# Spreading the conditioning products and the combination of the dilated branch over twice as many token steps

## Chip, cores and metric

The kernel runs on one core of a Trainium2 chip. The metric is the device time of one execution in microseconds, and lower is better. All data are float32. Matrix products run as three passes over operands that are split into a high part (`whi`, `hT0`) and a low part (`wlo`, `hT1`).

## What is computed

The reference is one encoder layer with conditioning. A vector `c` gives, through one large product, six rows that scale, shift and gate the two halves of the layer. The first half normalises the input, projects it, runs two kinds of attention side by side, gates and merges them; the second half is a SwiGLU network. Cut to what matters here:

```python
c_act = jax.nn.silu(c)
mod = c_act @ w_ada[l] + b_ada[l]
sh1, sc1, gt1, sh2, sc2, gt2 = jnp.split(mod, 6, axis=-1)
h = rms_norm(x, g_norm1[l]) * (1.0 + sc1) + sh1
proj = h @ w_in[l]                       # q, k, v of both branches, and the gates
o_a = neighbourhood_attention(qa, ka, va, rpb[l])
# dilated branch: three groups (dilation 1, 4, 16), each with its log-denominator
wts = jax.nn.softmax(jnp.stack(lses, axis=0), axis=0)
o_b = jnp.einsum('gbsh,gbshd->bshd', wts, jnp.stack(outs, axis=0))
gate_a, gate_b = jnp.split(jax.nn.sigmoid(gates + b_gate[l]), 2, axis=-1)
merged = gate_a * (o_a @ w_proj_a[l]) + gate_b * (o_b @ w_proj_b[l])
x = x + gt1 * (merged @ w_o[l])
# second half: SwiGLU with sh2, sc2, gt2
```

## The kernel before

The projections of the attention branches are made in ten units of eight token tiles of 128 tokens each. The main loop runs over steps `n` from 6 to 91, with `u, t = divmod(n, 8)`: unit and token tile. Units 0 to 5 belong to the three groups of the dilated branch, units 6 to 9 (n = 48 to 79) are the fourth kind, the neighbourhood attention. From n = 58 (`PAIRED`) on, each step takes the scores of one attention item, the product with the values of the item before last, and the transposes of the item in between. Steps n = 80 to 91 have no projection any more; in its place stand twelve blocks of the gate product (`gate_pre`), two blocks (the two halves of the tokens) for each pair of weight tiles.

One step is issued in this order. Four chunks of the projection (line 305) or of the gates (line 704); the attention: scores (L468), products with the values (L509), transposes of queries and keys (L369), transposes of the probabilities (L494); four more chunks; then `ada_step`, `combine_step`, and the work behind the projection, `proj_post`, which stores the values to `v_d` (L345). At the last tile of a unit the values are loaded back with eight DMAs (L358).

- `ada_step` takes one of 64 products of the conditioning. It is made on DVE: a block of weights `wa` (512 KB for two products, L288) times a column is added to an accumulator (L292, L294). After every eighth product `ada_row` sums the accumulator over the partitions with a product with ones on PE (L271), DVE adds the bias (L275), and the row is stored to `mod_d` (L276).
- The combination of the dilated branch has twelve blocks. `combine_prep(i)` loads a block of attention results `ut` (L643, L646, L650) and lets DVE spread the weights into `fb` (L655, two instructions). `combine_step(i)` transposes `fb` on PE (L664, four transposes into a bank of the tag `t`), and DVE multiplies (L672, or L674 and L675 with a sum). After six blocks the result goes to `o_d` (L677).
- The weights of the gates are loaded with L111, 256 KB each, into `raw`; ACT makes the high part (L118) and POOL the low part (L119).

Two shared things decide what can overlap. The PSUM tag `t` has two banks: L494, L664 and L271 take turns in them, so a bank has to be emptied by DVE or ACT before the next of them can start. The SBUF tag `raw` has six buffers: the weights of the gates (L111), `ut`, `fb`, `row` and `brow` all take their turn in this one ring, in the order in which the program asks for them.

PE runs in the order in which the code is written. The other engines and the DMA queue of SP are put into an order by a planner with priorities; each then runs strictly in its order, and an instruction that waits holds up all that stand behind it.

Of the kernel before, what the change touches and what calls it, by code (L numbers as in the profile page):

```python
# [36 lines left out]
PAIRED, RBT, COMB = 58, 5, 64  # L37
# [6 lines left out]
def hybrid_layer(ctx: ExitStack, tc: tile.TileContext, x, colp, wada1, wada2, bada2, wqkv, wg, wpa, wpb,  # L44
# [30 lines left out]
    def bank(tag):  # L75
        return ps.tile([128, 512], F32, tag=tag, name="ps_" + tag)
# [37 lines left out]
    def wsplit(r, eng=None):  # L114
        n = r.shape[1]
        hi = wp.tile([128, 512], F32R, tag="hi", bufs=NHL, name="whi")
        lo = wp.tile([128, 512], F32R, tag="lo", bufs=NHL, name="wlo")
        nc.scalar.activation(hi[:, :n], r, AF.Copy)  # L118
        (eng or nc.gpsimd).tensor_sub(lo[:, :n], r, fview(hi[:, :n]))  # L119
        return hi, lo  # L120
# [59 lines left out]
    def unit_load(u, k):  # L180
        return wload(wqkv[u, :, k, :], 384)
# [84 lines left out]
    ada_state = {"i": 0}  # L266
# [33 lines left out]
    def proj_chunk(U, t, k):  # L300
        if k == 0:
            U.pd[t] = bank("d" if U.u else "t")
        pd = U.pd[t]
        for i, (a, b) in enumerate(PASS):
            nc.tensor.matmul(pd[:, :384], tok(a, k, t), U.w[k][b][:, :384],  # L305
                             start=(k == 0 and i == 0), stop=(k == KT - 1 and i == 2))
# [89 lines left out]
    def new_unit(u, w):  # L396
        U = Unit()
        U.kind, U.pair = UNITS[u]
        U.u = u
        U.w = w  # L400
        U.pd, U.qn = {}, {}
        qk = ap_.tile([128, 4, S], F32R, tag="qk", bufs=2, name="qk")
        U.qk = [qk[:, i, :] for i in range(4)]
        if U.kind == 0:
            U.v = big("v", [128, 8, 128])
        if U.kind < 3:
            U.tab = rtab[0] if rtab else None
            U.st = ap_.tile([128, 9, 4], F32, tag="st", bufs=2, name="st")
        else:
            U.bias = []  # L410
        return U
# [116 lines left out]
    def cl_scores(C):  # L528
        C.pS = [bank("s") for _ in range(2)]
        for I in C.items:  # L530
            U, nq, nk = I.U, I.nq, I.nkb * 128
            for i, (a, b) in enumerate(PASS):
                for h in range(2):
                    hs = slice(h * 64, h * 64 + 64)
                    nc.tensor.matmul(C.pS[h][:nq, I.c0:I.c0 + nk], U.qk[a][hs, I.q0:I.q0 + nq],
                                     U.qk[2 + b][hs, I.kb0 * 128:I.kb0 * 128 + nk], start=(i == 0), stop=(i == 2))
# [122 lines left out]
    def combine_step(i):  # L659
        pr, g, hf = i // 6, (i % 6) // 2, i % 2  # L660
        fb, ut, uv, acc = cb[i]
        pf = bank("t")
        for j in range(4):
            nc.tensor.transpose(pf[:, j * 128:(j + 1) * 128], fb[:, j].rearrange("p h d -> p (h d)"), ident)  # L664
        acc = acc[:, hf * 512:hf * 512 + 512]
        n = 1 if g == 0 else (4 if g == 1 else 8)

        def v(z):
            return z if g == 0 else z.rearrange("p (i r) -> p i r", r=n)

        if g == 0:
            nc.vector.tensor_mul(acc, ut, pf)  # L672
        else:
            nc.vector.tensor_mul(v(pf), uv, v(pf))  # L674
            nc.vector.tensor_add(acc, acc, pf)  # L675
        if g == 2 and hf == 1:
            nc.sync.dma_start(o_d[4 + pr], cb[i][3])  # L677
# [14 lines left out]
    def gate_pre(n):  # L692

        i, br, hf = n // 4, (n // 2) % 2, n % 2
        hs = slice(hf * 512, hf * 512 + 512)
        st = {}

        def chunk(k):
            if k == 0:
                gate_w(i, br)  # L700
                st["p"] = bank("d")
            j, kk = divmod(k, 4)
            for q, (a, b) in enumerate(PASS):
                nc.tensor.matmul(st["p"], gw[i, br][j][a][:, kk * 128:(kk + 1) * 128], hT[b][:, k, hs],  # L704
                                 start=(k == 0 and q == 0), stop=(k == 7 and q == 2))
            if k == 7:
                if hf == 0:
                    gsig[i, br] = big("gsig")
                dst = gsig[i, br][:, hs]
                nc.scalar.activation(dst, st["p"], AF.Identity, bias=bg_c[:, 8 * br + i:8 * br + i + 1])  # L710
                nc.sync.dma_start(sig_d[i, br][:, hs], dst)

        return [lambda k=k: chunk(k) for k in range(8)]
# [200 lines left out]
    for n in range(6, 92):  # L914
        u, t = divmod(n, 8)
        if u < 10:
            if t == 0:
                units.append(new_unit(u, [nextw[u, k] for k in range(KT)]))
            U = units[u]
            chunks = [lambda k=k, U=U, t=t: proj_chunk(U, t, k) for k in range(KT)]  # L920
        elif n - 80 < NPRE:
            chunks = gate_pre(n - 80)
        else:
            chunks = []
        if u + 1 < 10:
            for k in ([0, 1, 2, 3, 4, 5, 6, 7] if n == 6 else [t] if u else []):
                raws[u + 1, k] = unit_load(u + 1, k)
            if t == 6:
                for k in range(2):
                    nextw[u + 1, k] = wsplit(raws[u + 1, k])  # L930
        if t == 2 and 1 <= u <= 10:
            for slot, I in unit_items(units[u - 1]):
                if I.U.kind < 3:
                    waiting.append(I)
                else:
                    ready.setdefault(8 * u + 2 + slot, []).append(I)
        if n == 8 * 7 + 5:
            combine_stats()
        ci = n - COMB
        if 0 <= ci < 12:  # L940
            combine_prep(ci)
        if n >= PAIRED:
            done, prev, cur = prev, cur, ready.pop(n, [])
        elif n % 2:
            done, prev, cur = prev, cur, []
            if waiting:
                cur = [Cluster()]
                while waiting and cur[0].keys + waiting[0].nkb * 128 <= 512:
                    cur[0].add(waiting.pop(0))
        else:  # L950
            done = []

        def chunk():
            if chunks:
                chunks.pop(0)()
                k = 8 - len(chunks)
                if t == 7 and u + 1 < 10 and k < 8 and k >= 2:
                    nextw[u + 1, k] = wsplit(raws[u + 1, k], nc.vector if k % 2 else None)

        turns = [(units[0], tt) for tt in {8: (0, 1), 9: (2, 3), 11: (4, 5), 13: (6, 7)}.get(n, ())]  # L960
        if PAIRED <= n <= 81 or 9 < n < PAIRED and n % 2:
            turns += [(units[m // 8], m % 8) for m in ((n - 2,) if n >= PAIRED else (n - 3, n - 2)) if m >= 8]
        chunk()
        chunk()
        chunk()
        chunk()
        if n < 10:
            while chunks:
                chunk()
        if n >= PAIRED or n % 2 or n < 10:  # L970
            for I in cur:
                if I.__class__ is Cluster:
                    cl_scores(I)
                    cl_qk(I)
                else:
                    at_scores(I)
                    at_qk(I, 0)
                    at_qk(I, 1)
            for I in done:
                (cl_pv if I.__class__ is Cluster else at_pv)(I)  # L980
            for j in range(0, len(turns), 2):
                qk_turns(turns[j:j + 2], "s" if n < 10 else "v")
            for I in prev:
                if I.__class__ is Cluster:
                    cl_turn(I)
                else:
                    at_turn(I, 0)
                    at_turn(I, 1)
        chunk()
        chunk()  # L990
        chunk()
        chunk()
        if n >= 8 and (t != 7 or u > 8) and ada_state["i"] < 65:
            ada_step()
        if 2 <= u < 6 and t < 5:
            if t in (2, 4):
                t_piece(2 * (u - 2) + t // 2 - 1, 2)
            if t in (0, 2):
                t_piece(2 * (u - 2) + t // 2, 0)
            if t in (1, 3):  # L1000
                t_piece(2 * (u - 2) + t // 2, 1)
        if n in (85, 88):
            w1_combos((n - 85) // 3, EARLY[(n - 85) // 3])
        if 1 <= ci < 13:
            combine_step(ci - 1)
        while chunks:
            chunk()
        if u < 10:
            proj_post(U, t)
            if U.kind == 3 and t == RBT:  # L1010
                bias_tabs(U)
# [646 lines left out]
```

## Time and profile before

| what | value |
|---|---|
| median of three runs | 1515.14 us (1513.23 to 1521.24) |
| profiled execution | 1508.57 us |
| its span, first to last instruction | 1506.8 us |
| PE busy | 1486.2 us, 99% |
| DVE busy | 1098.1 us, 73% |
| ACT busy | 656.3 us, 44% |
| POOL busy | 537.1 us, 36% |
| mean granted clock of PE | 0.999 |

The page counts an engine as busy from the start to the end of each instruction. PE is busy for nearly the whole span, so time can only be won where PE idles or runs at the lower clock, and it is lost wherever PE has to wait for something new. The steps that the change touches lie between about 360 us (n = 58) and 613 us (the end of n = 91); the gate blocks begin at 524.62 us.

### The profile page before, as it was taken

The numbers are of one execution on the slowest core, as the hardware profiler recorded it, in microseconds if no ns is written. First come the engines' busy times: TensorE is split into PE (matmuls) and PEld (weight loads), VectorE is DVE, ScalarE is ACT, GpSimd is POOL, SyncE is SP. The second block draws the span as 40 slices with busy tenths as digits, with TensorE's granted clock in tenths as the row PEclk, the third lists the DMA queues.
The fourth block names the chain that finished last, engine by engine and source line by source line (L and its number), as shares of the span: only waits on it lengthen the run. The fifth ranks groups of instructions, "written<-read, shape, count | busy, mean of one in ns | idle before, by whom it ended". The sixth has DMA issues, their size and how long they took to land. (4 is left out here: it accounts for less than half of the span.)

```text
span 1506.8 us, 24296 instructions
## 1 busy us (share of the span) xinstructions
PE 1486.2 (99%) x8156; PEld 1265.3 (84%) x8156; DVE 1098.1 (73%) x2318; ACT 656.3 (44%) x1638; POOL 537.1 (36%) x540
## 2 busy tenths in 40 slices
PE   9999999999999999999999999999999999999998
PEld 7999989998878877888888888888888888887886
DVE  6868777777889845466665597788767777599468
ACT  5655555555545543246432344233223323354442
POOL 0432333311100040002352301677767776104464
PEclk9999999999999999999999999999999999999999
DMA  9625444545145155834553225345433334798342
GB/s 371 226 85 186 141 153 143 192 137 166 59 126 169 62 179 154 318 98 126 168 188 137 92 90 186 119 131 182 155 127 108 109 105 147 268 380 280 98 150 102
DMA packets 154415, 241.66 MB, mean 160 GB/s; under 512 B 26657, under 2 KB 73377, under 8 KB 153521
## 3 DMA queue, kind: packets, MB, share of 16 engines
q1 hardware_dynamic: 153136, 235.90, 47.7%
q10 hardware_dynamic: 1152, 4.19, 0.7%
q8 instruction: 65, 1.06, 0.3%
q14 instruction: 62, 0.50, 0.1%
HBM read 179.89 MB, written 60.15 MB: 159 GB/s over the span
## 5 line engine op out<-in xcount | busy, mean ns | idle before, releaser
L119 POOL TENSOR_TENSOR wlo<-raw,whi 128x512 fp32r<-128x512 f32 (+2 forms) x133 | 172.5, 1310 | 463.4 <-ACT whi L118 435.3
L118 ACT ACTIVATE whi<-raw 128x512 fp32r<-128x512 f32 (+1 forms) x348 | 204.1, 599 | 260.0 <-PE ps_s L1493 35.4
L305 PE MATMUL ps_d<-whi,hT 128*128 128x384 f32 x1152 | 311.0, 341 | 0.0
L119 DVE TENSOR_TENSOR wlo<-raw,whi 128x512 fp32r<-128x512 f32 (+1 forms) x215 | 180.5, 852 | 75.2 <-ACT whi L118 70.8
L305 PEld LDWEIGHTS ps_d<-whi,hT 128*128 128x128 f32 x1152 | 210.3, 189 | 5.3 <-ACT vs L343 3.5
L305 PE MATMUL ps_d<-wlo,hT 128*128 128x384 f32 x576 | 193.6, 336 | 2.4 <-DVE wlo L119 2.0
L305 PEld LDWEIGHTS ps_d<-wlo,hT 128*128 128x128 f32 x576 | 108.9, 189 | 3.2 <-DVE wlo L119 2.3
L118 ACT ACTIVATE whi<-ws 128x512 fp32r<-128x512 f32 x65 | 40.8, 628 | 126.4 <-DVE ws L1340 74.2
L1273 POOL TENSOR_TENSOR e<-e,c 128x512 f32<-128x512 f32 x44 | 68.9, 1566 | 61.3 <-DVE c L1403 37.1
L335 POOL TENSOR_TENSOR ra<-qn,rtab 128x64 f32<-128x64 f32 x48 | 16.7, 348 | 153.4 <-DVE qn L328 138.4
L119 POOL TENSOR_TENSOR wlo<-m,whi 128x512 fp32r<-128x512 f32 x35 | 51.3, 1476 | 54.8 <-ACT whi L118 54.8
L1271 ACT ACTIVATE e<-e 128x512 f32<-128x512 f32 x44 | 27.5, 630 | 88.0 <-DVE e L1406 60.7
L547 ACT ACTIVATE P<-P,st 128x256 f32<-128x256 f32 (+2 forms) x100 | 45.5, 457 | 41.0 <-DVE st L545 41.0
L294 DVE SCALAR_TENSOR_TENSOR acc<-wa,cact,acc 128x512 f32<-128x512 f32 x56 | 43.2, 772 | 24.6 <-DMA wa<-in_wada_dram 24.6
L704 PE MATMUL ps_d<-hT,whi 128*128 128x512 f32 x192 | 60.6, 397 | 0.0
L483 ACT ACTIVATE P<-P,sx 128x384 f32<-128x384 f32 (+1 forms) x64 | 37.0, 580 | 51.4 <-DVE sx L482 51.4
L1323 PE MATMUL ps_v<-h2T,whi 128*128 128x512 f32 x192 | 59.2, 389 | 0.0
L1323 PE MATMUL ps_s<-h2T,whi 128*128 128x512 f32 x192 | 59.1, 389 | 0.0
L1323 PE MATMUL ps_d<-h2T,whi 128*128 128x512 f32 x184 | 56.7, 390 | 0.0
L129 ACT ACTIVATE ry<-ss,eps 128x4 f32<-128x4 f32 (+1 forms) x88 | 26.3, 299 | 69.5 <-DVE ss L326 67.2
L119 DVE TENSOR_TENSOR wlo<-ws,whi 128x512 fp32r<-128x512 f32 x45 | 50.3, 1117 | 8.2 <-ACT whi L118 8.1
L1272 DVE TENSOR_TENSOR e<-e 128x512 f32<-128x512 f32 x44 | 42.5, 974 | 17.3 <-ACT e L1271 17.2
(445 smaller groups left out, 3951.6 us busy)
## 6 DMA issues: line engine op xcount, KB each, us to landing
raw<-in_w_dram SPq DMA_DIRECT2D x139, 256.0 KB
ga_d<-e SPq DMA_DIRECT2D x77, 256.0 KB
raw<-ga_d SPq DMA_DIRECT2D x77, 256.0 KB
wa<-in_wada_dram SPq DMA_DIRECT2D x32, 512.0 KB
raw<-in_wqkv_dram SPq DMA_DIRECT2D x80, 192.0 KB
m<-in_w_dram SPq DMA_DIRECT2D x44, 256.0 KB
raw<-in_wg_dram SPq DMA_DIRECT2D x42, 256.0 KB
xt<-in_x_dram SPq DMA_DIRECT2D x16, 512.0 KB
```

What stands on the lines that cost most here:

```text
L118: nc.scalar.activation(hi[:, :n], r, AF.Copy)
L119: (eng or nc.gpsimd).tensor_sub(lo[:, :n], r, fview(hi[:, :n]))
L129: nc.scalar.activation(y, ss, AF.Ln, scale=1.0 / n, bias=eps)
L294: nc.vector.scalar_tensor_tensor(ada_acc[c], wa, cact[:, kk:kk + 1], ada_acc[c], op0=ALU.mult, op1=ALU.add)
L305: nc.tensor.matmul(pd[:, :384], tok(a, k, t), U.w[k][b][:, :384], start=(k == 0 and i == 0), stop=(k == KT - 1 and i == 2))
L483: nc.scalar.activation(P[:nq, :nk], P[:nq, :nk], AF.Exp, scale=-1.0, bias=nm, accum_out=sm)
L547: nc.scalar.activation(C.P[h][:nq, c], C.P[h][:nq, c], AF.Exp, scale=-1.0, bias=nm, accum_out=sm)
L704: nc.tensor.matmul(st["p"], gw[i, br][j][a][:, kk * 128:(kk + 1) * 128], hT[b][:, k, hs], start=(k == 0 and q == 0), stop=(k == 7 and q == 2))
L1271: nc.scalar.activation(sg, a, AF.Sigmoid)
L1272: nc.vector.tensor_mul(sg, sg, a)
L1273: nc.gpsimd.tensor_mul(sg, sg, up)
L1323: nc.tensor.matmul(pb, w[p][:, k * 128:(k + 1) * 128], b[q][:, k], start=(k == 0 and i == 0), stop=(k == 3 and i == 2))
```

## The change

The number of products and blocks stays the same; their steps change.

- Conditioning: before, every step from n = 8 takes one product, but for the last tile of units up to 8; all are done by n = 80. Now, from n = 58, only even steps take one, up to n = 76; from n = 77 every step takes one, and the last (with its row) stands in n = 87.
- Combination: before, blocks are prepared at n = 64 to 75 and taken one step later, at 65 to 76. Now they are prepared at the even steps 64 to 86 and taken at the odd steps 65 to 87.

```diff
-        ci = n - COMB
-        if 0 <= ci < 12:
+        ci, odd = divmod(n - COMB, 2)
+        if 0 <= ci < 12 and not odd:
             combine_prep(ci)
...
-        if n >= 8 and (t != 7 or u > 8) and ada_state["i"] < 65:
+        if n >= 8 and (n % 2 == 0 or n > 76 if n >= PAIRED else t != 7) and ada_state["i"] < 65:
             ada_step()
...
-        if 1 <= ci < 13:
-            combine_step(ci - 1)
+        if 0 <= ci < 12 and odd:
+            combine_step(ci)
```

What this does to the order of the engines is shown at three places. Names carry the program's buffer numbers, which differ between the two programs; `wa2` is `wa`, `acc2` the accumulator of the conditioning.

**First block of the combination, on DVE** (n = 65 and 66). Before, `ps_t_6248` is the bank of the first block and L672 empties it:

```order
L486 TENSOR_SCALAR P_6198<-P_6198,sx_6199 128x256
L393 SCALAR_TENSOR_TENSOR qk_5323<-ps_v_6214,hg_87,qk_5323 128x2x64
L394 TENSOR_TENSOR qk_5323<-ps_v_6214,qk_5323 128x2x64
L294 SCALAR_TENSOR_TENSOR acc2_5912<-wa2_6245,cact_100,acc2_5912 128x512 x2
L672 TENSOR_TENSOR oacc_6064<-ut_6065,ps_t_6248 128x512
L326 TENSOR_REDUCE ss4_6258<-sq_6255 128x4
```

Now, `ps_t_6228` is the bank of the same block:

```order
L486 TENSOR_SCALAR P_6181<-P_6181,sx_6182 128x256
L393 SCALAR_TENSOR_TENSOR qk_5323<-ps_v_6197,hg_87,qk_5323 128x2x64
L394 TENSOR_TENSOR qk_5323<-ps_v_6197,qk_5323 128x2x64
L672 TENSOR_TENSOR oacc_6052<-ut_6053,ps_t_6228 128x512
L326 TENSOR_REDUCE ss4_6238<-sq_6235 128x4
```

The two products L294 that stood ahead of L672 have gone from here.

**The seam between the last projection and the first gate block, on PE** (n = 79 and 80). `whi_7792` and `whi_7735` are the high parts of the same first gate weights, `wlo` their low parts. Before:

```order
L305 MATMUL ps_d_7687<-wlo_6921,hT0_112 128x384
L305 MATMUL ps_d_7687<-whi_6920,hT1_406 128x384
L704 MATMUL ps_d_7802<-hT0_112,whi_7792 128x512
L704 MATMUL ps_d_7802<-hT1_406,whi_7792 128x512
L704 MATMUL ps_d_7802<-hT0_112,wlo_7793 128x512
```

Now:

```order
L305 MATMUL ps_d_7609<-wlo_6869,hT0_112 128x384
L305 MATMUL ps_d_7609<-whi_6868,hT1_406 128x384
L271 MATMUL ps_t_7683<-acc2_6341,ones_94 1x512
L664 MATMUL ps_t_7694<-ident_89,fb_7512 128x128 x4
L704 MATMUL ps_d_7745<-hT0_112,whi_7735 128x512
L704 MATMUL ps_d_7745<-hT1_406,whi_7735 128x512
L704 MATMUL ps_d_7745<-hT0_112,wlo_7736 128x512
```

A row sum of the conditioning and a block of the combination have moved in between.

The queue of SP around the loads of these weights (`raw_7790` and `raw_7796` before, `raw_7733` and `raw_7739` now). Before:

```order
L345 DMA v_d_76<-vs_7180 128x128
L416 DMA rb_7589<-in_rbias_dram 128x768
L513 DMA o_d_75<-stg_7228 128x128
L288 DMA wa2_7665<-in_wada2_dram 128x1024
L111 DMA raw_7790<-in_wg_dram 128x512
L345 DMA v_d_76<-vs_7286 128x128
L111 DMA raw_7796<-in_wg_dram 128x512
```

Now:

```order
L513 DMA o_d_75<-stg_7649 128x128
L646 DMA ut_7728<-u_d_74 128x4x128
L345 DMA v_d_76<-vs_7716 128x128
L276 DMA mod_d_72<-row_7685 1x512
L111 DMA raw_7733<-in_wg_dram 128x512
L358 DMA v_7719<-v_d_76 128x1x128 x8
L111 DMA raw_7739<-in_wg_dram 128x512
```

Before, the stores of values (L345) of six steps stood between the first load and the eight value loads L358 that follow the last store; the weights were asked for 35 us ahead of their use (489.34 to 524.62 us). Now the first load stands behind the row of the seam itself, and it waits for the transposes L664 of the seam, which give back the buffer of `fb_7512`; the second stands behind the eight value loads.

**The seam between the fourth and the fifth pair of gate weights** (n = 87 and 88). PE before:

```order
L704 MATMUL ps_d_8352<-hT1_406,whi_8278 128x512
L704 MATMUL ps_d_8352<-hT0_112,wlo_8279 128x512
L704 MATMUL ps_d_8433<-hT0_112,whi_8423 128x512
L704 MATMUL ps_d_8433<-hT1_406,whi_8423 128x512
L704 MATMUL ps_d_8433<-hT0_112,wlo_8424 128x512
```

PE now:

```order
L704 MATMUL ps_d_8337<-hT0_112,wlo_8263 128x512
L271 MATMUL ps_t_8406<-acc2_7692,ones_94 1x512
L664 MATMUL ps_t_8413<-ident_89,fb_8251 128x128 x4
L704 MATMUL ps_d_8433<-hT0_112,whi_8423 128x512
L704 MATMUL ps_d_8433<-hT1_406,whi_8423 128x512
```

SP before, where `raw_8421` is the load that `whi_8423` is made from:

```order
L111 DMA raw_8270<-in_wg_dram 128x512
L111 DMA raw_8276<-in_wg_dram 128x512
L513 DMA o_d_75<-stg_7926 128x128
L111 DMA raw_8421<-in_wg_dram 128x512
L111 DMA raw_8427<-in_wg_dram 128x512
```

SP now:

```order
L711 DMA sig_d_77<-gsig_8333 128x512
L513 DMA o_d_75<-stg_8377 128x128
L711 DMA sig_d_77<-gsig_8333 128x512
L111 DMA raw_8421<-in_wg_dram 128x512
L276 DMA mod_d_72<-row_8408 1x512
L111 DMA raw_8427<-in_wg_dram 128x512
```

The load has moved behind the second store of the gates of n = 87 (`sig_d`, L711), which waits until ACT has emptied the bank of that step's last product (L710).

## Rows read from the trace of the kernel before

**Rows 1.** The page: busy time, share and instructions of each engine.

```profile
PE 1486.2 (99%) x8156; PEld 1265.3 (84%) x8156; DVE 1098.1 (73%) x2318; ACT 656.3 (44%) x1638; POOL 537.1 (36%) x540
```

**Rows 2.** Stretches: length, busy PE, PEld, DVE, ACT, POOL; clock, DMA, GB/s.

```profile
410.00:430.00 20.00, 16.35 (x119) 14.35 (x118) 14.74 (x58) 9.62 (x36) 0.00 (x0) 1.00 0.59 188
...
470.00:490.00 20.00, 18.80 (x135) 16.29 (x133) 17.50 (x61) 9.53 (x34) 0.00 (x0) 1.00 0.68 202
490.00:510.00 20.00, 19.00 (x138) 16.15 (x138) 19.49 (x63) 9.38 (x31) 2.99 (x2) 1.00 0.29 95
...
530.00:550.00 20.00, 20.00 (x115) 15.11 (x115) 8.24 (x24) 10.21 (x25) 10.23 (x9) 1.00 0.67 204
```

**Rows 3.** Waits, 360 to 512 us: us in total, times, longest.

```profile
PE ps_t L494 <- DVE oacc L672: 2.3, 1, 2.3
...
PE ps_t L664 <- ACT PT L500: 1.4, 2, 1.1
...
PE ps_t L494 <- DVE oacc L675: 1.2, 1, 1.2
```

**Rows 4.** Timeline at the first combination block: start, duration, engine, line, operation.

```profile
418.62 0.42 SPq L288 DMA_DIRECT2D wa<-in_wada_dram  x1
...
423.69 1.54 DVE L294 SCALAR_TENSOR_TENSOR acc<-wa,cact,acc 128x512 f32<-128x512 f32 x2 [3.98 <-DMA wa<-in_wada_dram]
425.14 0.68 DVE L672 TENSOR_TENSOR oacc<-ut,ps_t 128x512 f32<-128x512 f32 x1
...
425.88 0.44 PE L494 MATMUL ps_t<-ident,P 128*128 128x128 f32 x2 [2.33 <-DVE oacc L672]
...
429.48 0.66 PE L664 MATMUL ps_t<-ident,fb 128*128 128x128 f32 x4 [1.05 <-ACT PT L500]
```

**Rows 5.** Three stretches with PE's granted clock (PEclk), columns as in rows 2.

```profile
366.00:373.50 7.50, 5.24 (x31) 4.01 (x29) 5.77 (x19) 2.99 (x12) 0.00 (x0) 1.00 0.99 391
373.50:376.90 3.40, 3.40 (x13) 3.40 (x12) 3.40 (x15) 1.43 (x5) 0.00 (x0) 0.50 0.09 31
...
423.00:426.00 3.00, 0.67 (x5) 0.43 (x6) 2.28 (x4) 0.00 (x0) 0.00 (x0) 1.00 0.68 259
```

**Rows 6.** Timeline of SP's queue, 484 to 545 us.

```profile
489.34 0.43 SPq L111 DMA_DIRECT2D raw<-in_wg_dram  x1
...
525.67 0.32 SPq L345 DMA_DIRECT2D v_d<-vs  x1
527.28 4.94 SPq L358 DMA_DIRECT2D v<-v_d  x8
...
534.03 0.38 SPq L111 DMA_DIRECT2D raw<-in_wg_dram  x1
534.61 0.23 SPq L276 DMA_DIRECT2D mod_d<-row  x1
```

**Rows 7.** Timeline at the first gate blocks, all engines, 524 to 540 us.

```profile
524.62 0.63 PE L704 MATMUL ps_d<-hT,whi 128*128 128x512 f32 x2
...
527.47 0.79 PE L468 MATMUL ps_s<-qk 64*128 64x384 f32 x6
...
529.84 0.71 PE L704 MATMUL ps_d<-hT,whi 128*128 128x512 f32 x2
...
532.79 1.02 PE L271 MATMUL ps_t<-acc,ones 128*1 128x512 f32 x2
532.90 0.69 ACT L710 ACTIVATE gsig<-ps_d,cp 128x512 f32<-128x512 f32 x1 [1.78 <-PE ps_d L704]
...
533.74 0.73 PE L704 MATMUL ps_d<-hT,whi 128*128 128x512 f32 x2
...
539.06 1.25 ACT L118 ACTIVATE whi<-raw 128x512 fp32r<-128x512 f32 x2 [5.47 <-DMA raw<-in_wg_dram]
...
539.77 1.30 POOL L119 TENSOR_TENSOR wlo<-raw,whi 128x512 fp32r<-128x512 f32 x1 [42.57 <-ACT whi L118]
```

**Rows 8.** Timeline: a later load of gate weights (SP), and ACT waiting for it.

```profile
543.66 0.33 SPq L111 DMA_DIRECT2D raw<-in_wg_dram  x1
...
546.95 0.63 ACT L118 ACTIVATE whi<-raw 128x512 fp32r<-128x512 f32 x1 [0.40 <-DMA raw<-in_wg_dram]
```

## The prediction, made before the changed kernel ran

> **What bounds the kernel now.** I read the page first: PE is busy for 99% of the span [rows 1], so the end is set by PE's own work plus what PE idles, and every saving has to be an idle stretch of PE. The change adds and removes no product, so PE's busy time stays. Next come the stretches of 20 us through the steps that change [rows 2]: the reader is to see that PE idles 20.00 - 16.35 = 3.65 us in 410 to 430, 1.20 in 470 to 490, 1.00 in 490 to 510, and nothing from 530 on, where the gate blocks run. In 490 to 510 DVE is busy for 19.49 of 20 us: there it has nothing to spare. The waits say who is late [rows 3]: PE's transposes of the probabilities (L494) wait for DVE's L672 or L675, which empty the bank of a combination block, and a block's own transposes wait for ACT's L500.
>
> The timeline shows the largest one [rows 4]. A load of `wa` is issued at 418.62; the first product that needs it, L294, starts only at 423.69, after 3.98 us in which DVE does nothing, and L672, queued behind two such products, at 425.14. PE's L494 waits 2.33 us for it; the next block then waits another 1.05 us behind the late ACT. One more idle stretch lies ahead of the combination: 366.00 to 373.50 has 5.24 us of busy PE, and right after it the granted clock is 0.50, the lower level of 1.2 GHz, for 3.40 us [rows 5]. The idle stretch of 423 to 426, with 0.67 busy of 3.00, was not followed by such a fall; the clock is 1.00 over all of 410 to 430 [rows 2].
>
> **Gain: the token steps.** In the new order no L294 stands ahead of L672 of the first block, so the wait of 2.33 us goes; the second block moves two steps further and the wait of 1.05 us behind it goes with it. The small waits of 470 to 510 come from a full DVE. One L294 (0.77 us, half of the pair in [rows 4]) and a block's own work on DVE (0.68 us in L672 alone) move out of every second step, so DVE gets room. All of it is 3.65 + 1.20 + 1.00 = **5.85 us**, the upper end. Around n = 73 the new order still has two products next to a block's L674 and L675, and a wait of 0.27 us (the rest of the 3.65 after 2.33 and 1.05) hangs on another copy; I leave 0.85 us and take **-5.0** (range -5.85 to -4.0). The idle stretch before 373.50 stays, lower clock and all: the products and loads there keep their order.
>
> **Cost 1: the seam at n = 80.** The moved blocks keep the ring `raw` busy until n = 87, and the gate weights queue in the same ring. Before, the first load of them went out at 489.34 [rows 6], 35 us ahead of its use at 524.62 [rows 7]. Now it goes out after the seam's own instructions, and PE reads it right behind them. Let 0 be the start of L271 at the seam, the place of 524.62 before.
> - PE has L271, 0.95 us (532.79 to 533.74), and the four transposes, 0.66 [rows 4, 7]: it is free at 1.61.
> - SP first sends `mod_d`, which waits for L271 and DVE's sum: 534.61 - 532.79 = 1.82 [rows 6, 7]. The issue takes 0.23, so the load goes out at 2.05. It also waits for the transposes, done at 1.61, which is earlier.
> - From issue to use a 256 KB load of these weights took 534.03 to 539.06 = 5.03 us with much in the queue [rows 6, 7] and 543.66 to 546.95 = 3.29 in a quieter place [rows 8]. The queue at the seam is short but not empty; I take 4.0.
> - ACT makes the high part in 0.63 (half of 1.25). PE starts at 2.05 + 4.0 + 0.63 = 6.68: an idle stretch of 6.68 - 1.61 = **5.07 us**.
> - The third product needs the low part. POOL starts 0.71 after ACT and takes 1.30, so it comes 2.01 after ACT starts [rows 7], 1.38 after PE's start. PE reaches it after two products, some 0.47 us later: **0.9 us**.
> - The second load stands behind the eight value loads. Counted from the same point, the last store goes out at 525.67 - 524.62 = 1.05, the value loads from 527.28 - 524.62 = 2.66 to 7.60 [rows 6, 7]; the weights land at 11.6, the low part is there at 13.6. PE needs it after its first four chunks (2.85, from 524.62 to 527.47, and 0.9), the attention (2.37, from 527.47 to 529.84) and two products: at 6.68 + 2.85 + 0.9 + 2.37 + 0.47 = 13.27. So **0.3 us** more.
>
> Together **6.3 us**; with landings of 3.3 and 5.0 us it is 5.6 and 7.3. Queued behind these waits on ACT are the first exponentials of n = 80; their transposes are due a step later, 8.2 us (524.62 to 532.79) [rows 7], which covers them.
>
> **Cost 2: the seam at n = 88.** `raw_8421` stands behind the second `sig_d`. Again from the start of L271: ACT empties the last bank from 0.11 to 0.80 (532.90 + 0.69), `sig_d` follows, and the load behind it went out at 534.03 - 532.79 = 1.24 in the place before [rows 6, 7]. PE is free at 1.61 and starts at 1.24 + 4.0 + 0.63 = 5.87: **4.26 us**, and **0.9** for the low part: **5.2** (4.5 to 6.2). The second load follows at once and has four chunks of cover. The pairs for n = 82, 84, 86 and 90 go out a step or more ahead, so I cost them at nothing; the cover is the two blocks of the pair before, about 16 us at 8.2 us each.
>
> **The clock.** A fall to 0.50 for 3.40 us costs half, 1.70 us, less what PE stands anyway for the low part: (3.40 - 0.9) / 2 = 1.25 at each seam. Whether it comes is open: one stretch with PE idle for 2.26 us in pieces was followed by it, one with 2.33 in one piece was not [rows 5]. The seams idle twice as long as either. Bounds 0 and 2 x 1.70 = 3.4; I take **1.3**.
>
> **Sum.** -5.0 + 6.3 + 5.2 + 1.3 = **+7.8 us**. The profiled execution took 1508.57 us, 6.57 below the median, so an execution like it would take 1516.4, and the median becomes 1515.14 + 7.8 = **1522.9**. All good ends give -5.85 + 5.6 + 4.5 = +4.3 (1519.4); all bad ends -4.0 + 7.3 + 6.2 + 3.4 = +12.9 (1528.0). The bound of 0.5%, about what a measurement of this kernel can tell from no change, is 7.6 us: the sum lies on it.
>
> The Trainium skill ("DMA: Bandwidth & Descriptors", "Rules for kernel authors") advises to issue a transfer early and wait for it late, since the fixed cost then overlaps; moving the gate loads next to their use goes against that. The same page ("Anatomy of one DMA") fits one transfer as 2.0 us plus bytes over 436 GB/s, which would be an estimate of 2.6 us for 256 KB; by it the two seams would cost 2.8 us less and the sum be +5.0. Both landings of these weights in the trace, 3.29 and 5.03 us, are longer, and they decide.
>
> **Rivals.**
> 1. *The waits stay, the clock doesn't fall, the loads land quickly.* Price as above: +4.3 to +6.5, so 1519.4 to 1521.6, within 0.5% and not slower by the bound. It is decided by whether the load comes nearer 3.3 than 5.0 us after its issue and whether the granted clock stays 1.00 at both seams. For it: the queue is emptier at the seams than at 534, and the stretch of 423 to 426 kept its clock. Chance 0.43.
> 2. *Forecast: the waits at the two seams with at least one fall of the clock, or slow landings.* +7.6 to +13. For it: a stretch of 5 us without a matmul is far longer than 2.33. The Trainium skill ("TensorE: Matmul & The Clock Gate", "HAM oscillation") describes this: long waits for loads send the array back to half clock, and the work behind them starts slow. By that rule both seams fall, 2 x 1.25 = 2.5 in place of 1.3: +9.0, 1524.1. No wait that long is in this trace. Chance 0.43.
> 3. *Only the relief shows.* If PE found its weights ready at both seams, the time would fall by 4.0 to 5.85, to 1509.3 to 1511.1. It needs loads that go out some 5 us before the seams end, and the order puts them behind the seams' own instructions, so it would take another mechanism than I see, such as relief of DVE worth more than PE's idle time shows. Chance 0.09.
> 4. *The change doesn't do what it says.* The planner sets DVE's order by priorities, not by steps; if products bunch up beside the blocks again, the idle 2.2 us of 470 to 510 stay and only 3.4 are won: +1.6 on the sum, 1524.5. Against it: DVE's work per pair of steps does fall. Chance 0.05, slower.
>
> **How the numbers follow.** Slower by over 0.5%: 0.43 + 0.05 = 0.48; within: 0.43; faster: 0.09. The range takes the bounds 1519.4 and 1528.0, reaches down to 1514 for half of the relief with cheaper seams, and up to 1530 for waits in the queue of DVE at n = 81 to 87 that the trace of before can't show. About 1 in 10 stays out on either side.
>
> **What would show it.** In the profile after: no wait of L494 for L672 near 423 us; PE's idle time in 410 to 430 near zero; the first L704 waiting some 5 us on ACT's L118, itself on the load; the same some 60 us later, a little shorter; a granted clock near 0.50 just behind either. I am wrong if PE's first L704 starts within 2 us of L664, or if waits of over 1 us appear between 525 and 620 at other lines.

## The result and the profile after

The changed kernel takes 1521.78 us (median of 20 runs, 1519.08 to 1524.22), the kernel before 1514.25 us (20 runs, 1509.64 to 1521.24). The ratio is 1.0049 with a 95% interval of 1.0039 to 1.0059: slower by 7.5 us. The prediction was +7.8 us, with the relief of the token steps and the waits at both seams as its parts.

The page of the profiled execution (1521.33 us), with PE's row under the span:

```profile
span 1519.2 us, 24284 instructions
...
PE 1492.3 (98%) x8156; PEld 1270.8 (84%) x8156; DVE 1097.4 (72%) x2318; ACT 655.6 (43%) x1638; POOL 538.9 (35%) x540
```

The stretches that answer to [rows 2] (length, busy PE, PEld, DVE, ACT, POOL, granted clock, DMA share, GB/s):

```profile
410.00:430.00 20.00, 19.77 (x136) 17.03 (x136) 17.19 (x65) 10.31 (x38) 0.06 (x1) 1.00 0.46 137
...
470.00:490.00 20.00, 20.00 (x152) 18.14 (x151) 18.36 (x68) 10.68 (x40) 0.00 (x0) 1.00 0.34 101
490.00:510.00 20.00, 20.00 (x149) 17.96 (x148) 16.60 (x57) 9.97 (x35) 0.00 (x0) 1.00 0.36 114
510.00:530.00 20.00, 15.34 (x83) 10.94 (x83) 9.66 (x33) 6.75 (x20) 2.56 (x2) 0.83 0.35 102
...
590.00:610.00 20.00, 14.85 (x79) 10.79 (x79) 8.27 (x18) 8.55 (x17) 10.42 (x8) 0.83 0.74 224
```

The 5.85 us in which PE idled in the first three of these stretches have shrunk to 0.23. In their place stand two holes, 4.66 us in 510 to 530 and 5.15 us in 590 to 610, each with a mean clock of 0.83. PE's waits from 360 to 620 us name them (total, times, longest; [rows 3] before):

```profile
PE ps_d L704 <- ACT whi L118: 9.5, 2, 5.0
PE ps_t L494 <- DVE P L486: 2.2, 3, 0.8
...
PE ps_t L494 <- DVE oacc L675: 0.4, 1, 0.4
```

L672 has gone from the list. The first seam in the timeline, to be read against [rows 6, 7]:

```profile
517.79 0.66 PE L664 MATMUL ps_t<-ident,fb 128*128 128x128 f32 x4
...
518.60 0.24 SPq L276 DMA_DIRECT2D mod_d<-row  x1
...
518.93 0.35 SPq L111 DMA_DIRECT2D raw<-in_wg_dram  x1
...
519.38 4.90 SPq L358 DMA_DIRECT2D v<-v_d  x8
...
522.29 0.63 ACT L118 ACTIVATE whi<-raw 128x512 fp32r<-128x512 f32 x1 [3.94 <-DMA raw<-in_wg_dram]
...
522.98 1.22 PE L704 MATMUL ps_d<-hT,whi 128*128 128x512 f32 x2 [4.53 <-ACT whi L118]
...
524.32 0.46 SPq L111 DMA_DIRECT2D raw<-in_wg_dram  x1
```

The load goes out 0.48 us after PE has ended the transposes, ACT has it 3.36 us later, and PE has stood 4.53 us. The second seam:

```profile
590.25 0.66 PE L664 MATMUL ps_t<-ident,fb 128*128 128x128 f32 x4
...
590.53 0.38 SPq L111 DMA_DIRECT2D raw<-in_wg_dram  x1
...
595.24 1.32 ACT L118 ACTIVATE whi<-raw 128x512 fp32r<-128x512 f32 x2 [5.15 <-DMA raw<-in_wg_dram]
595.92 1.22 PE L704 MATMUL ps_d<-hT,whi 128*128 128x512 f32 x2 [5.02 <-ACT whi L118]
```

Here the load needs 4.71 us. The granted clock around both (columns as above):

```profile
518.40:522.00 3.60, 0.05 (x1) 0.00 (x0) 3.50 (x13) 0.00 (x0) 0.00 (x0) 1.00 0.40 117
522.00:522.98 0.98, 0.00 (x1) 0.01 (x1) 0.03 (x1) 0.63 (x1) 0.00 (x0) 0.51 0.42 124
522.98:528.85 5.87, 5.74 (x12) 3.65 (x12) 0.00 (x0) 0.63 (x1) 1.57 (x2) 0.50 0.63 186
...
593.70:595.90 2.20, 0.00 (x0) 0.00 (x0) 0.00 (x0) 0.63 (x1) 0.00 (x0) 0.50 1.04 381
595.90:600.50 4.60, 4.44 (x10) 3.05 (x11) 0.00 (x0) 3.07 (x5) 4.55 (x4) 0.50 0.87 310
```

The clock falls while PE still stands, and the first 5.87 and 4.60 us of gate products run at 0.50.

**Where the time went, stage by stage.** The table gives the time between starts of PE instructions, PE's idle time in brackets. Seam 80 runs from the last L305 to the first L704 of n = 81, seam 88 from the last L704 of n = 87 to the first of n = 89. The third column of times is the kernel before once more, the last one the changed kernel with both gate loads early; both are told of below.

| stage | before | changed | before, second profile | gate loads early |
|---|---|---|---|---|
| start to n = 58 | 361.66 | 363.25 | 363.77 | 363.31 |
| n = 58 to 61 | 28.71 (2.26) | 29.45 (2.99) | 30.53 (3.14) | 31.09 (3.32) |
| n = 62 to 79 | 134.07 (5.87) | 123.87 (0.65) | 137.92 (8.38) | 125.53 (1.87) |
| seam 80 | 9.30 (0) | 17.55 (4.66) | 9.29 (0) | 9.79 (0) |
| n = 81 to 87 | 53.51 (0) | 54.85 (0) | 53.51 (0) | 55.31 (0.23) |
| seam 88 | 8.02 (0) | 17.27 (5.15) | 8.02 (0) | 9.60 (0) |
| n = 89 to the end | 906.66 | 908.06 | 907.53 | 908.85 |

Some of it is moved work. With the loads early, seam 80 holds one combination block more than before and nothing else, so a block is 9.79 - 9.30 = 0.49 us of PE. Five blocks and one row sum (0.95) leave n = 62 to 79: 3.4 us. Of the -10.20 there, -6.8 are relief. Against the last column, with the same work in each stage, the waits at the seams cost 17.55 - 9.79 = 7.76 and 17.27 - 9.60 = 7.67 us, 15.4 together. The two spans lie only 10.9 us apart (1519.2 and 1508.3): the kernel with early loads takes 4.6 us longer in the other stages, 3.3 of them in n = 58 to 79.

The spans of the changed kernel and of the first profile of before lie 12.4 us apart, the medians only 7.5: the first profile of before (1508.57) lies below the lowest of its 20 runs. The first experiment shows what was missing from it.

### The profile page after: what moved, and what is told of

The parts are those of the page before. It is cut to its first block, busy times and chain, and to the rows that moved or that the text cites. A ratio compares the mean times of both kernels' runs of the same rounds, so it can differ in the third digit from the quotient of the medians.

```text
span 1519.2 us, 24284 instructions
## 1 busy us (share of the span) xinstructions
PE 1492.3 (98%) x8156; PEld 1270.8 (84%) x8156; DVE 1097.4 (72%) x2318; ACT 655.6 (43%) x1638; POOL 538.9 (35%) x540
## 3 DMA queue, kind: packets, MB, share of 16 engines
q8 instruction: 65, 1.06, 0.3%
## 4 chain that ended last, share of the span: by engine, by line
PE 80%; DVE 7%; DMA 7%; ACT 2%; issue 2%; POOL 1%; SPq 1%; DVEq 0%; POOLq 0%; ACTq 0%
PE ps_d L305 14%; PE ps_v L1323 7%; PE ps_d L1323 7%; PE ps_s L1323 7%; PE ps_t L1323 6%; PE ps_d L704 4%; PE ps_s L1493 3%; PE ps_d L1493 3%; PE ps_s L1258 2%; PE ps_d L1258 2%; PE ps_t L1493 2%; PE ps_v L1493 2%; DVE wlo L119 2%; DMA m<-in_w_dram 2%; PE ps_v L1258 1%
## 5 line engine op out<-in xcount | busy, mean ns | idle before, releaser
L305 PE MATMUL ps_d<-whi,hT 128*128 128x384 f32 x1152 | 310.3, 341 | 0.0
L305 PEld LDWEIGHTS ps_d<-whi,hT 128*128 128x128 f32 x1152 | 210.6, 189 | 5.2 <-ACT vs L343 3.5
L305 PE MATMUL ps_d<-wlo,hT 128*128 128x384 f32 x576 | 194.1, 337 | 2.2 <-DVE wlo L119 1.8
L305 PEld LDWEIGHTS ps_d<-wlo,hT 128*128 128x128 f32 x576 | 109.1, 189 | 3.0 <-DVE wlo L119 2.2
L704 PE MATMUL ps_d<-hT,whi 128*128 128x512 f32 x192 | 64.3, 418 | 9.5 <-ACT whi L118 9.5
L294 DVE SCALAR_TENSOR_TENSOR acc<-wa,cact,acc 128x512 f32<-128x512 f32 x56 | 42.1, 751 | 26.5 <-DMA wa<-in_wada_dram 26.3
L704 PEld LDWEIGHTS ps_d<-hT,whi 128*128 128x128 f32 x192 | 36.9, 200 | 17.1 <-ACT whi L118 10.0
```

The lines of the kernel that those rows point to most:

```text
L294: nc.vector.scalar_tensor_tensor(ada_acc[c], wa, cact[:, kk:kk + 1], ada_acc[c], op0=ALU.mult, op1=ALU.add)
```

## Experiments

**Theory:** DVE's order is freed of products that wait for their load, which gives 5 us or more, and the ring of `raw` buffers makes the gate loads late, which costs more. **Rivals:** the waits would only move to another place if the loads were early; the blocks in the gate steps cost by themselves; the clock falls for another reason than PE's standing.

**The kernel before, unchanged, with a second profile.**

> The kernel before itself, unchanged, with a second profile. The profiles of before and of the changed kernel lie 12.4 us apart, the medians 7.5. Theory: the first profile of before was one of its quicker executions, without the lower clock that the changed kernel and all others show near 214 us, in code that is the same in all; then this profile shows that stretch of 0.50 near 214 us and a span of 1509 to 1514 us, and the ratio is 1.000 +- 0.0015. Rival: that stretch comes from the changed order and is a cost of the change; then it is absent here again.

Ratio 1.0010 (0.9994 to 1.0027), median 1515.89 us, profiled 1517.23. First the stretch near 212 us in the first profile of before:

```profile
212.00:216.00 4.00, 2.43 (x14) 2.40 (x14) 3.93 (x12) 1.22 (x5) 0.00 (x0) 1.00 0.27 77
```

The same stretch, the next 3 us, and two stretches within the token steps in the second profile of before:

```profile
212.00:216.00 4.00, 2.53 (x9) 2.53 (x10) 3.93 (x13) 1.21 (x5) 0.00 (x0) 0.74 0.29 84
216.00:219.00 3.00, 3.00 (x27) 2.63 (x27) 1.79 (x7) 0.50 (x2) 2.08 (x8) 0.78 0.07 22
...
490.00:510.00 20.00, 16.23 (x103) 14.52 (x104) 19.10 (x57) 8.20 (x28) 3.00 (x2) 0.91 0.33 99
...
493.81:497.22 3.41, 3.41 (x14) 3.32 (x13) 3.05 (x14) 1.30 (x5) 0.00 (x0) 0.50 0.44 145
```

Its largest waits of PE from 360 to 620 us, and then, from the timeline, DVE at the first block:

```profile
PE ps_t L494 <- DVE oacc L675: 3.3, 1, 3.3
PE ps_t L494 <- DVE oacc L672: 3.1, 1, 3.1
```

```profile
428.37 1.54 DVE L294 SCALAR_TENSOR_TENSOR acc<-wa,cact,acc 128x512 f32<-128x512 f32 x2 [4.78 <-DMA wa<-in_wada_dram]
```

The lower clock near 214 us belongs to the kernel before too and is no cost of the change. And the same program waits 3.1 us for L672 and 3.3 for L675 here, where the first profile had 2.3 and 1.2 [rows 3], because DVE stands longer at the loads of `wa`: 4.78 us instead of 3.98 [rows 4] at the first block. Behind the wait of 3.3 us the clock falls as well (the stretch from 493.81). The relief is therefore 6.8 us against the first profile and 137.92 - 123.87 - 3.4 = 10.7 against the second. The span was 1515.4 us, above the 1509 to 1514 expected.

**Both gate loads early.** The first and the fifth pair take their ring turn ahead of the blocks:

```diff
+        if n in (76, 86):
+            gate_w((0, 2)[n == 86], 0)
         ci, odd = divmod(n - COMB, 2)
```

> The changed kernel, but the first and the fifth pair of gate weights take their turn in the buffer ring at n = 76 and n = 86, ahead of the blocks prepared there, so that their loads go out many microseconds before use. Theory (the change wins 5 to 6 us in the token steps and loses more at the two seams, where PE waits for these loads and then runs at the lower clock): no wait of L704 for L118 at either seam, clock 1.00 there, and the time falls below the kernel before by 5 to 7 us, ratio 0.9955 +- 0.0015. Rival (the waits only change places: PE is next held by the split of later weights, by ACT's queue or by DVE): new waits of some 5 us between 515 and 620 us and a ratio of 1.002 to 1.005, like the changed kernel.

Ratio 0.9974 (0.9963 to 0.9985), 1510.09 us: 4 us faster than before. The two stretches with the seams:

```profile
510.00:530.00 20.00, 20.00 (x136) 16.30 (x133) 15.81 (x56) 9.35 (x32) 0.00 (x0) 1.00 0.32 100
580.00:600.00 20.00, 20.00 (x131) 14.86 (x130) 9.67 (x24) 8.81 (x20) 7.70 (x6) 1.00 0.57 173
```

PE never idles there and the clock stays at 1.00. So it is the late loads that make the changed kernel slow. The gain is a little under the 5 to 7 us expected. Two other rows of this profile, a wait of PE and a stretch:

```profile
PE ps_t L664 <- ACT PT L500: 1.0, 1, 1.0
```

```profile
374.81:381.63 6.82, 6.00 (x20) 5.61 (x21) 6.29 (x22) 3.36 (x12) 0.00 (x0) 0.50 0.05 16
```

The wait is new: the transposes of the block of n = 73 start 1.0 us late (478.97). The changed kernel has no such wait; this one has it, and so have the three kernels below that keep the steps of the change and load the first pair early (0.96 to 0.97). The early loads are thus not quite free, though nothing like the 5 us of the rival. In n = 58 to 61, which the change doesn't mend, this profile idles 1.06 us longer than the first one of before, and the clock stays at 0.50 for 6.82 us behind it instead of 3.40 [rows 5].

**Only the first of them early.** As above without the call at n = 86.

> The changed kernel with only the first pair of gate weights asked for early, at n = 76; the seam at n = 88 is left as it is. Theory (the seams cost the same and independently, 7.8 and 7.7 us by the profiles of the changed kernel and of the one with both loads early): half of the way between these two, ratio to before 1.001 +- 0.0015, the wait of 5 us and the lower clock only at n = 88. Rival (one seam's wait is what the other seam's relief brings back, as PE catches up with later work): the time of the changed kernel, or that of the one with both early.

Ratio 1.0012 (1.0003 to 1.0021), 1514.84 us. Its largest wait from 360 to 620 us:

```profile
PE ps_d L704 <- ACT whi L118: 4.7, 1, 4.7
```

Seam 80 takes 9.79 us, seam 88 17.59. From 1.0049 over 1.0012 to 0.9974 each seam is worth 0.0037 or 0.0038 of the time, some 5.7 us; the intervals allow about 2 us either way, so the profiles' 7.7 lies at their edge. Within these 2 us the seams add up independently.

**PE kept busy at the seams.** Behind the blocks of n = 79 and 87:

```diff
+        if n in (79, 87):
+            pw = bank("v")
+            for i in range(KEEP):        # KEEP = 38
+                nc.tensor.transpose(pw[:, :128], ident, ident)
```

> The changed kernel with 38 idle transposes of the identity on PE at each of the two seams, right behind the block's transposes and ahead of the first product that waits for the weights; nothing reads them, and they take about 4 us each time, less than PE waits there. Theory (the clock fell because PE did nothing for about 5 us): the granted clock stays 1.00 behind both seams, the low part of the weights now shows as a wait of up to 0.9 us at each, and the time is 3 to 5 us under the changed kernel, ratio to before 1.002 to 1.003. Rival (the clock falls for another reason, or such transposes don't count): clock 0.50 again behind both seams and the time of the changed kernel, 1.005, or more.

Ratio 1.0038 (1.0023 to 1.0054), 1520.9 us. Lines are one higher here; L1010 are the idle transposes:

```profile
521.68 4.31 PE L1010 MATMUL ps_v<-ident 128*128 128x128 f32 x38
...
526.38 0.73 PE L705 MATMUL ps_d<-hT,whi 128*128 128x512 f32 x2 [0.38 <-ACT whi L119]
...
527.73 0.50 PE L705 MATMUL ps_d<-hT,wlo 128*128 128x512 f32 x1 [0.62 <-POOL wlo L120]
```

The stretches behind both seams:

```profile
523.00:530.00 7.00, 6.00 (x40) 4.85 (x38) 2.33 (x8) 0.63 (x1) 1.27 (x1) 1.00 0.51 136
...
596.00:604.00 8.00, 6.87 (x50) 5.08 (x49) 1.25 (x5) 3.60 (x6) 4.81 (x4) 1.00 0.89 295
```

The clock stays 1.00: it fell because PE stood still. But the low part now comes late, 0.62 us at the first product that needs it (the row of L705 that waits for POOL) and as much at two more places. And PE still waits 0.38 and 0.51 us for the high part. Seam 80 takes 16.60 us and seam 88 15.41, together 2.8 less than in the changed kernel, not 3 to 5. In the time alone this doesn't stand out: the intervals of 1.0038 and 1.0049 overlap.

**Only the combination spread** (the conditioning line as before):

> Only the combination is spread; the conditioning products stay at every step. In this order the first gate weights go out two steps ahead and nothing stands before the fifth pair, while the two products L294 stay ahead of L672 of the first block. Theory: the wait of 2.3 us of L494 for L672 stays near 423 us, the waits behind later blocks shrink, no wait at either seam: 1 to 3.5 us faster than before, ratio 0.998 to 0.9995. Rival (the combination's blocks at odd steps past n = 79 are what costs, by their own work in the gate steps): slower than before by 2 us or more even with the weights in time.

Ratio 1.0030 (1.0017 to 1.0043), slower, against the theory's 1 to 3.5 us faster. PE's waits from 360 to 620 us, and then, from the timeline, DVE at the largest:

```profile
PE ps_t L494 <- DVE oacc L675: 3.7, 1, 3.7
PE ps_t L494 <- DVE oacc L672: 2.8, 1, 2.8
PE ps_t L664 <- DVE PT L498: 2.3, 2, 1.7
```

```profile
575.18 0.69 DVE L759 TENSOR_TENSOR w1m<-w1m 128x512 f32<-128x512 f32 x1 [3.71 <-DMA w1m<-in_w_dram]
```

The wait for L672 stays, with two L294 ahead of it, as expected: the spread of the products is what removes it in the changed kernel. The weights are in time, but at n = 79 the block's own transposes wait 1.7 us for DVE's L498 (the third row), which I had not expected. The larger surprise is the 3.7 us from 579 us on. In the gate steps DVE stands at a load of `w1m`; as long as no block had to be emptied there this hurt nobody, but a block of the combination moved to n = 85 is queued behind it. So the rival holds in part: a block in the gate steps can cost, though not by its own 0.49 us. In the changed kernel DVE stands at these loads for 1.3 us at most, and n = 81 to 87 have no idle time.

**Only the conditioning spread** (the combination as before):

> Only the conditioning products are spread; the combination stays at n = 64 to 76. In this order no L294 stands ahead of L672 of the first block, the first gate weights go out before the seam at n = 80, but the load for n = 88 still stands behind the store of the gates of n = 87. Theory: the wait of 2.3 us near 423 us goes, one seam wait of about 5 us with a lower clock behind it (2 to 2.5 us) comes at n = 88: within 0.3% of before, from -1 to +5 us. Rival (it is the combination that holds the ring at both seams): no wait at n = 88, 3 to 5 us faster than before.

Ratio 1.0050 (1.0034 to 1.0066), some 7 us slower; up to 5 were expected. Its first waits:

```profile
PE ps_d L704 <- ACT whi L118: 5.9, 2, 4.9
PE ps_t L494 <- DVE P L486: 3.2, 3, 2.1
PE ps_s L468 <- DVE sx L482: 2.8, 2, 2.2
```

The wait for L672 is gone, and seam 88 is there with 4.9 us (17.13 us in all), without any block beside it: the moved row sum is enough. Seam 80 has a wait of 1.1 us for the first weights and one of 0.6 for their low part. The longest waits for DVE, 2.2 us near 370 and 2.1 near 616 us, I can't assign to the edit.

**No products at n = 58 to 61, and none from 56 on.** PE idles in n = 58 to 61 in every kernel. On top of early gate loads (at 76, 86 and 88):

```diff
-(n % 2 == 0 or n > 76 if n >= PAIRED else t != 7)
+(n % 2 == 0 and n > 61 or n > 74 if n >= PAIRED else t != 7)    # first
+(n % 2 == 0 and n > 61 or n > 72 if n >= 56 else t != 7)        # second
```

> All three pairs of gate weights that follow moved work asked for early (n = 76, 86, 88), and no conditioning products at n = 58 to 61; the even steps from 62 and every step from 75 take them. Theory (the wait and the lower clock near 372 us come from DVE holding products that wait for a late load ahead of the probabilities): the idle time of PE between n = 58 and n = 62 falls from about 3 us to under 1.5, 1 to 3 us faster than the kernel with the loads early, ratio to before 0.9955 to 0.997. Rival (the products there are late ones of earlier steps, and PE waits all the same): idle time of 3 us and 0.9975.

> As the kernel without products at n = 58 to 61, but none at n = 56 and 57 either; every step from 73 takes one. Theory: the wait near 372 us goes altogether, clock 1.00 there, 2 to 5 us faster than the kernel with the loads early, ratio to before 0.9945 to 0.9965. Rival (the products pushed into n = 73 to 79 fill DVE again beside the blocks): new waits of 1 to 3 us between 470 and 515 us that give it back, 0.997 to 0.999.

Ratios 1.0026 (1.0015 to 1.0038) and 1.0048 (1.0036 to 1.0060): both slower than with the gate loads early alone. The first does what it should in its place: idle time in n = 58 to 61 falls to 1.48 us and the clock stays there (in the second it is 1.73). A row of DVE's timeline further on, and PE's waits from 360 to 620 us:

```profile
568.03 2.18 DVE L294 SCALAR_TENSOR_TENSOR acc<-wa,cact,acc 128x512 f32<-128x512 f32 x2 [4.56 <-DMA wa<-in_wada_dram]
```

```profile
PE ps_t L494 <- DVE oacc L675: 3.5, 3, 2.3
PE ps_t L664 <- DVE PT L498: 3.2, 2, 3.0
PE ps_t L494 <- DVE row L275: 2.0, 1, 2.0
```

The products have taken their late loads with them: behind the one that waited 4.56 us stands the L498 for which PE's L664 waits 3.0. The second has the same 3.0 us and a wait of 5.4 us for the second pair of gate weights at n = 82: there a row sum has moved next to the block that stands ahead of those loads. The third pair of gate weights, early in both, was not tried by itself.

**Earlier loads instead of fewer products.** If the late load is the cause, asking for it earlier should help without any spreading. The edit asks for each load of `wa` LEAD products ahead: on the kernel before with a lead of two, and on the one with early gate loads with leads of one and two.

```diff
-        if kk % 2 == 0:
-            ada_acc["w"] = big("wa2", [128, 2, 512])
-            nc.sync.dma_start(ada_acc["w"], wada2[c, :, kk:kk + 2, :])
-        wa = ada_acc["w"][:, kk % 2, :]
+        for j in ((i + LEAD,) if i else range(LEAD + 1)):
+            if j % 2 == 0 and j < 64:
+                ada_acc["w", j // 2] = big("wa2", [128, 2, 512])
+                nc.sync.dma_start(ada_acc["w", j // 2], wada2[j // 8, :, j % 8:j % 8 + 2, :])
+        wa = ada_acc["w", i // 2][:, kk % 2, :]
```

> The kernel before with one edit: each load of conditioning weights is asked for two products earlier, so that its buffer turn and its place in SP's queue come earlier; steps of products and blocks as before. Theory (the waits of the token steps come from DVE standing at a product whose load went out only 4 to 5 us earlier, not from the number of products per step): the wait near 425 us shrinks to under 1 us, 2 to 5 us faster than before, ratio 0.997 to 0.9985, without any seam. Rival (DVE is simply full there, and only fewer products per step help): waits of 1 us and more stay behind the blocks, 0.999 to 1.001.

> The changed kernel with the first and fifth pair of gate weights asked for early, and each load of conditioning weights asked for one product earlier. Theory: with the loads ahead, the products no longer hold up the probabilities near 372 us; idle time of PE from n = 58 to 79 falls from 5.2 us to under 3, ratio to before 0.9945 to 0.9965. Rival (the ring of large buffers, not the order, decides when these loads go out): idle time as with the gate loads early alone, 0.997 to 0.998.

> As the kernel with a lead of one product, with a lead of two. Theory: as there or better, 0.994 to 0.9965, idle time under 3 us from n = 58 to 79. Rival (the buffer ring decides): 0.997 to 0.998, idle time of 4 to 5 us.

The kernel before with a lead of two: 0.9966 (0.9953 to 0.9978), 1510.3 us. DVE's timeline at the first block, and PE's waits from 360 to 620 us (lines one higher):

```profile
422.96 1.54 DVE L295 SCALAR_TENSOR_TENSOR acc<-wa,cact,acc 128x512 f32<-128x512 f32 x2 [0.44 <-DMA wa<-in_wada_dram]
```

```profile
PE ps_t L495 <- DVE P L487: 2.2, 3, 1.2
PE ps_t L495 <- DVE oacc L676: 0.7, 1, 0.7
```

The same two products stand ahead of the same block, every step still takes one, and the wait for L672 has gone, since DVE stands 0.44 us at them where it stood 3.98 [rows 4] and 4.78. So here the number of products per step was not the main thing; when the load comes was. With the gate loads early as well, a lead of one gives 0.9954 (0.9939 to 0.9970; 1508.36 us) and a lead of two 0.9959 (0.9945 to 0.9973; 1508.25 us), 6 to 7 us faster than before and the quickest of all here. The time came as the theory said, the idle time of n = 58 to 79 didn't: 4.71 and 4.27 us instead of under 3. There the loads still go out behind the eight value loads; no experiment frees them. Whether these two differ from the 0.9974 without a lead is not settled: the intervals overlap.

## Why the prediction came out right

- **What bounds the kernel, and the place of the gain:** right. L672 is no longer waited for, and the idle time of 410 to 510 is nearly gone, as [rows 2 to 4] said.
- **Size of the gain (-5.0, range -5.85 to -4.0):** by the profiles too small. It is -6.8 against the profile that I had and -10.7 against the second one. I counted idle time alone, and that fell by 5.22; the other 1.6 us are busy time of PE, and no run shows what they come from. And one profile showed one sample of waits that hang on when a load lands: in the other two of them were 3.1 and 3.3 us instead of 2.3 and 1.2, and behind the second the clock fell too. One reading of the change was wrong without harm: the second block moves one step further (n = 66 to 67), not two; its wait of 1.05 us has gone all the same.
- **The stretch before 373.50 stays:** right; 2.26 us of idle time became 2.99.
- **Cost 1 (6.3):** the mechanism and the order of events were right. The idle time was 4.53, not 5.07, as the load landed 3.36 us after its issue, near the lower of my two rows, not 4.0. The waits for low parts (0.9 and 0.3) hardly came, 0.13: at half clock PE is slow enough for POOL to keep up (with transposes in the gap and the clock at 1.00 it was 0.62 each time). The estimate of 2.6 us by the Trainium skill ("DMA: Bandwidth & Descriptors", "Anatomy of one DMA") does not serve here: that fit is for transfers issued from GpSimd, these are issued from SP, and 3.36 and 4.71 us were measured from issue to use.
- **Cost 2 (5.2):** 5.02 us of idle time, not 4.26; the load landed after 4.71 us. Low part 0.14, not 0.9.
- **The clock (1.3, bounds 0 and 3.4):** the term that was mis-sized. It fell at both seams, and for twice as long as in [rows 5]: 5.74 and 4.44 us of busy PE ran at 0.50, and half of that is 2.9 and 2.2, 5.1 together, above my upper bound. The price of a seam less its idle time says much the same: 7.76 - 4.66 = 3.1 and 7.67 - 5.15 = 2.5 us, together 5.6. With the low parts, which lie in the idle time, it is 5.9 against 1.3 + 0.9 + 0.3 + 0.9 = 3.4. The Trainium skill's passage ("TensorE: Matmul & The Clock Gate", "HAM oscillation"), which I gave as a rule for both seams, agrees with the trace: 0.50 behind waits of 4.53 and 5.02 us.
- **The sum:** -5.0 + 12.8 = +7.8 was forecast. By the profiles the seams are 15.4, with -6.8 of relief against them and 0.7 more in n = 58 to 61 by the first profile of before, +9.3, and with -10.7 and -1.1 by the second, +3.6. The measured +7.5 lies between. By the times the parts come out nearer to the forecast: the kernel with both gate loads early is 3.9 us faster than before (1.7 to 5.6), and from there to the changed kernel it is 0.0075 of the time, 11.4 us, with about 2 us either way. Which of the two accounts is the better one these intervals don't settle. That the total was met within 0.3 us is partly luck: by the profiles two terms were 2 to 6 us too small, on opposite sides.
- **Rivals:** that the clock doesn't fall and the loads land quickly (1) is out, although one load did land near 3.3 us and the time lies within the 0.5% that went with it. The mechanism is that of (2), and its price, +7.6 to +13, begins just above the measured +7.5: the interval of the ratio, 1.0039 to 1.0059, has the bound of 0.5% inside it. PE found its weights ready (3) only in the kernel with both loads early, which is 3.9 us faster, about the lower end of the 4.0 to 5.85 named. That the products bunch up again (4) didn't happen.

## What to carry to other kernels

When work is moved, list what shares a buffer ring with it and see which load now gets its turn later: here a few row sums and blocks, worth 0.5 to 1 us each, pushed the 256 KB loads of two pairs of gate weights right next to their use and cost some 11 us by the times, 15 by the profiles. An in-order engine that stands at a load holds up everything queued behind it, so look for the load that goes out late before spreading the work; asking for it two products earlier won as much as the spread with its gate loads early (ratios 0.9966 and 0.9974, overlapping intervals), without moving any product. And take waits that hang on when a load lands from more than one profile.

## What the chip showed that I had not expected

The granted clock fell while PE stood still at the seams, 3.6 us (518.4 to 522.0) and 2.8 us (590.9 to 593.7) after its last product, and stayed at 0.50 for some 6.8 us, twice the 3.40 of [rows 5]. The wait of 2.0 us at 211 us that both profiles of before share was followed by 0.50 in the second profile of before and not in the first. With transposes that compute nothing in the gap the clock stayed at 1.00.
